# Token scaling by a diagonal matmul instead of a scaled transpose, with the norm's weights applied at the PSUM exit

## The chip, the cores and the metric

The kernel runs on one core of one Trainium2 chip. The metric is the device time of one execution in microseconds (us). A profiled execution also gives a span, from its first to its last recorded instruction.

## The reference, cut to what matters

One layer of a streaming encoder is computed for 512 prompt tokens and 64 sample tokens (576 together), each 1024 channels wide. Everything begins with one norm, whose result feeds a projection with some 13,000 columns:

```python
def _rmsnorm(x, w):
    y = x * lax.rsqrt(jnp.mean(x * x, axis=-1, keepdims=True) + EPS)
    return y * w

h = _rmsnorm(x, norm_pre_w)          # (tokens, 1024)
proj = h @ w_in                      # split into the inputs of three branches
```

The branches (a gated convolution of width 31, a state-space scan with a convolution of width 4 ahead of it, and a cross-attention) are gated, added, projected by `w_out`, normed and added to x. Only the norm at the very start is touched here.

## The kernel before, in words

**What is kept.** TensorE wants h with channels on the partitions. `hT` holds it so: 8 blocks of 128 channels by 576 tokens, once as a rounded half `hT[0]` and once as the remainder `hT[1]` (both in the type fp32r). A projection (`mac`, L218) multiplies each weight block in three parts: high weights by high h, high weights by low h, low weights by high h.

**The start.** Tokens come in five tiles, four of 128 rows and one of 64. For each, L266 issues the load of 128 x 1024 values on the SP queue. Behind the first stands L270, which loads the norm's weights repeated on all 128 partitions (`wpre`); behind the second, `prep_to(1)` issues the loads of the first two weight blocks, named B0 and C0 (L183). ScalarE rounds each weight block to its high half (`whi`, L193) and VectorE subtracts for the low half (`wlo`, L195).

**One token tile, `x_tr(t)`.** ScalarE squares the tile and sums along the row (L274) and takes the root (L275). VectorE inverts it (L276) and multiplies the tile by that column and by `wpre` in one instruction (L280). TensorE transposes eight 128 x 128 blocks into two PSUM banks, four to a bank (L291). For each bank ScalarE copies 128 x 512 into `hT[0]` (L295), and VectorE subtracts to give `hT[1]` (L296).

**The order at the start** is written out by hand, and the matmuls in it are pinned in this order:

```python
    warm_pe(16)
    x_tr(0)
    warm_pe(6)
    x_tr(1)
    warm_pe(6)
    first_mac(0, "B0")          # tokens of tiles 0 and 1
    x_tr(2)
    first_mac(0, "C0", 0, 4)
    x_tr(3)
    first_mac(0, "C0", 4, 8)
    x_tr(4)
```

Then follow the second halves (320 tokens of tiles 2, 3 and 4) of B0 and C0. `warm_pe(n)` issues n plain fp32 matmuls of the 128 x 128 identity with itself (L303); nobody reads them. PSUM tiles named `ps` come from a pool of four.

**What is not pinned** (ScalarE, VectorE, GpSimd, SP and the other matmuls) is put in order ahead of time by a planner, which walks the program by priority with costs of its own. At run time each engine takes its instructions strictly in that order.

**What comes after.** Small parameters are loaded as rows and transposed: eight of them into `vraw` (L424), transposed at L437; the weights and the state of the width-4 convolution (`scw`, `sts`) by `load_t`, through a tile `praw` with the tag `bt` of the pool `sc` (L431 load, L433 transpose, L434 copy). The tag `bt` has two buffers. The tile `after`, used by `dt_cum` (L404), has the same tag and holds one of them until then. `conv4` (L454) takes B0, C0 and then x0 to x3 through that convolution: its first ScalarE step L466 needs `scw` and, by a GpSimd copy (L459), `sts`. Beside it `dt_soft` runs a chain of small VectorE steps, whose last (L394) is what the first matmul of `dt_cum` (L402) reads. That matmul is pinned behind the projection x3. Afterwards come the chunks of the scan, with projections filled in between.

Of the kernel before, what the change touches and what calls it, by code (L numbers as in the profile page):

```python
# [8 lines left out]
F32 = mybir.dt.float32  # L9
F32R = mybir.dt.float32r  # L10
AF = mybir.ActivationFunctionType
ALU = mybir.AluOpType
# [6 lines left out]
D = 1024  # L19
# [9 lines left out]
def hybrid_trunk_kernel(  # L29
# [9 lines left out]
    nc = tc.nc  # L39
# [5 lines left out]
    const = ctx.enter_context(tc.tile_pool(name="const", bufs=1))  # L45
# [11 lines left out]
    def ps_tile():  # L57
        return pp_[1].tile([128, 512], F32, tag="ps", name="ps")


    ident = const.tile([128, 128], F32, name="ident")
# [19 lines left out]
    hT = [big.tile([128, KD, T], F32R, name=f"hT{i}") for i in range(2)]  # L81
# [156 lines left out]
    def v2(ap):  # L238
# [7 lines left out]
    sc = stc.enter_context(tc.tile_pool(name="sc", bufs=2, reuse_waits="tile"))  # L246
# [8 lines left out]
        out=mask, in_=mask, pattern=[[1, 128]], compare_op=ALU.is_ge, fill=0.0,  # L255
# [3 lines left out]
    xt = []  # L259
    for t in range(5):  # L260
        n = 128 if t < 4 else 64
        if t < 4:
            x_t = obf[:, D * t:D * t + D]
        else:
            x_t = sc.tile([128, D], F32, tag="M", name="x4")
        nc.sync.dma_start(out=x_t[:n], in_=xp_d[128 * t:128 * t + 128] if t < 4 else xs_d)  # L266
        xt.append((x_t, n))
        if t == 0:
            wpre = sc.tile([128, D], F32, tag="R", name="wpre")
            nc.sync.dma_start(out=wpre, in_=norm_pre_w[0].partition_broadcast(128))  # L270
        if t == 1:
            prep_to(1)
    def rms_tile(x_t, n, sq, ss, w):
        nc.scalar.activation(sq[:n], x_t[:n], AF.Square, accum_out=ss[:n, 0:1])  # L274
        nc.scalar.activation(ss[:n, 1:2], ss[:n, 0:1], AF.Sqrt, scale=1.0 / D, bias=eps1[:n])  # L275
        nc.vector.reciprocal(ss[:n, 2:3], ss[:n, 1:2])  # L276
        if w is None:
            nc.vector.tensor_scalar(x_t[:n], x_t[:n], ss[:n, 2:3], None, ALU.mult)
        else:
            nc.vector.scalar_tensor_tensor(x_t[:n], x_t[:n], ss[:n, 2:3], w[:n], ALU.mult, ALU.mult)  # L280

    sqx = sc.tile([128, D], F32, tag="M", name="sqx")
    ssx = const.tile([128, 5, 4], F32, name="ssx")
    def x_tr(t):
        x_t, n = xt[t]
        rms_tile(x_t, n, sqx, ssx[:, t], wpre)
        for b in range(2):
            p = ps_tile()
            for k in range(4):
                kc = 512 * b + 128 * k  # L290
                m = nc.tensor.transpose(p[:, n * k:n * k + n], x_t[:n, kc:kc + 128], ident[:n, :n])  # L291
                tc.keep_in_program_order(m)
            v = p[:, :4 * n].rearrange("p (k t) -> p k t", k=4)
            d = slice(128 * t, 128 * t + n)
            nc.scalar.activation(hT[0][:, 4 * b:4 * b + 4, d], v, AF.Copy)  # L295
            nc.vector.tensor_tensor(  # L296
                hT[1][:, 4 * b:4 * b + 4, d], v, hT[0][:, 4 * b:4 * b + 4, d].bitcast(F32), ALU.subtract
            )

    def warm_pe(n):  # L300
        p = ps_tile()
        for _ in range(n):
            tc.keep_in_program_order(nc.tensor.matmul(p[:, 0:128], lhsT=ident, rhs=ident, start=True, stop=True))  # L303
# [9 lines left out]
        )  # L313

    pt0 = {"B0": mm_tile(), "C0": mm_tile()}
    warm_pe(16)
    x_tr(0)
    warm_pe(6)
    x_tr(1)
# [11 lines left out]
    def tr_act(tiles, k, dst, wcol, ncols):  # L331
# [18 lines left out]
        out=after, in_=after, pattern=[[-1, 128]], compare_op=ALU.is_ge, fill=0.0,  # L350
# [85 lines left out]
    p = ps_tile()  # L436
# [406 lines left out]
    for kp in range(2):  # L843
# [16 lines left out]
        a, b = blk(0, 1), blk(0, 0)  # L860
        nc.vector.tensor_tensor(b, b, a, ALU.subtract)
        put("T1", b)
        c = blk(1, 1)
# [4 lines left out]
        d = blk(1, 0)  # L868
# [650 lines left out]
```

## Time and profile before

| what | value |
|---|---|
| median of 3 runs | 1129.82 us (1129.18 to 1131.78) |
| the profiled execution | 1130.53 us, span 1128.8 us |
| TensorE matmul, weight load | busy 97% and 93% of the span |
| VectorE, ScalarE, GpSimd | busy 76%, 54%, 12% |
| granted TensorE clock, mean | 0.989 |

In a row of the timeline stand the start, the time until the last of the merged instructions ended, the engine, the line, the operation, output and inputs, the count, and in brackets how long the engine had been idle and what ended that. "SPq" is the queue that issues loads. An fp32 matmul is recorded as two instructions (two passes): the 28 matmuls of `warm_pe` are 56 records at L303. Transposes and fp32r matmuls are one record each.

### The profile page before, as it was taken

The numbers are of one execution on the slowest core, as the hardware profiler recorded it, in microseconds if no ns is written. First come the engines' busy times: TensorE is split into PE (matmuls) and PEld (weight loads), VectorE is DVE, ScalarE is ACT, GpSimd is POOL, SyncE is SP. The second block draws the span as 40 slices with busy tenths as digits, with TensorE's granted clock in tenths as the row PEclk, the third lists the DMA queues.
The fourth block names the chain that finished last, engine by engine and source line by source line (L and its number), as shares of the span: only waits on it lengthen the run. The fifth ranks groups of instructions, "written<-read, shape, count | busy, mean of one in ns | idle before, by whom it ended". The sixth has DMA issues, their size and how long they took to land.

```text
span 1128.8 us, 20472 instructions
## 1 busy us (share of the span) xinstructions
PE 1091.0 (97%) x8081; PEld 1047.3 (93%) x8081; DVE 862.8 (76%) x1370; ACT 607.7 (54%) x1069; POOL 133.2 (12%) x230
## 2 busy tenths in 40 slices
PE   8999999999999999968998999999999999999997
PEld 8999999999999999968998999999899999999974
DVE  5778898578867878796888989849788789475533
ACT  5654675456437642362666576656445733674331
POOL 0100120012002100012121331100000111111000
PEclk9999999999999999988999999999999999999999
DMA  7354433442354633473867767757556889868912
GB/s 206 95 156 124 138 114 104 127 117 80 95 144 112 149 96 99 113 172 74 191 177 203 161 145 199 208 164 198 151 155 159 185 225 223 201 161 184 252 39 84
DMA packets 202213, 168.74 MB, mean 149 GB/s; under 512 B 15014, under 2 KB 175822, under 8 KB 202118
## 3 DMA queue, kind: packets, MB, share of 16 engines
q1 hardware_dynamic: 188294, 128.77, 39.4%
q0 software_dynamic: 12096, 35.13, 17.2%
q10 hardware_dynamic: 1728, 3.54, 0.8%
q8 instruction: 63, 1.03, 0.4%
q14 instruction: 32, 0.26, 0.1%
HBM read 117.08 MB, written 15.21 MB: 117 GB/s over the span
## 4 chain that ended last, share of the span: by engine, by line
PE 85%; DVE 6%; DMA 4%; ACT 2%; issue 1%; SPq 0%; DVEq 0%; ACTq 0%; POOLq 0%
PE mm L218 51%; PE X L950 9%; PE Y L950 5%; PE ps L218 4%; PE ps L1165 2%; PE ps L1166 2%; PE Z L950 2%; PE ps L1164 2%; PE ps L577 2%; PE ps L603 1%; PE ps L581 1%; DVE c L760 1%; DMA ob<-in_x_prompt_dram 1%; PE ps L542 1%; DMA wlo<-raw 1%
## 5 line engine op out<-in xcount | busy, mean ns | idle before, releaser
L218 PE MATMUL mm<-hT,whi 128*128 128x288 f32 (+2 forms) x2240 | 399.4, 298 | 1.7 <-ACT ob L689 0.7
L218 PEld LDWEIGHTS mm<-hT,whi 128*128 128x128 f32 x2240 | 334.2, 189 | 5.6 <-issue 2.2
L218 PE MATMUL mm<-hT,wlo 128*128 128x288 f32 (+2 forms) x1120 | 246.2, 298 | 0.0
L193 ACT ACTIVATE whi<-raw 128x1024 fp32r<-128x1024 f32 x118 | 124.7, 1057 | 196.5 <-PE mm L218 166.1
L760 DVE SCALAR_TENSOR_TENSOR c<-u,dww,c 128x606 f32<-128x606 f32 x240 | 202.1, 845 | 2.3
L218 PEld LDWEIGHTS mm<-hT,wlo 128*128 128x128 f32 x1120 | 184.7, 189 | 0.8 <-issue 0.6
L218 PE MATMUL mm<-hi,whi 128*128 128x288 f32 x512 | 112.2, 301 | 8.1 <-ACT hi L620 7.8
L195 DVE TENSOR_TENSOR wlo<-raw,whi 128x1024 fp32r<-128x1024 f32 x68 | 83.0, 1220 | 41.4 <-ACT whi L193 41.4
L218 PE MATMUL mm<-lo,whi 128*128 128x288 f32 x512 | 110.8, 298 | 1.6 <-DVE lo L622 1.6
L218 PE MATMUL mm<-hi,wlo 128*128 128x288 f32 x512 | 110.6, 297 | 0.8 <-DMA wlo<-raw 0.8
L218 PEld LDWEIGHTS mm<-hi,whi 128*128 128x128 f32 x512 | 83.1, 191 | 9.4 <-ACT hi L620 8.1
L198 POOL DMA_DIRECT2D wlo<-raw x50 | 43.9, 878 | 389.5 <-ACT wlo L197 286.7
L218 PEld LDWEIGHTS mm<-lo,whi 128*128 128x128 f32 x512 | 83.4, 190 | 1.9 <-DVE lo L622 1.9
L218 PEld LDWEIGHTS mm<-hi,wlo 128*128 128x128 f32 x512 | 83.2, 189 | 1.2 <-DMA wlo<-raw 1.0
L197 ACT ACTIVATE wlo<-raw 128x1024 fp32r<-128x1024 f32 x50 | 52.4, 1048 | 21.9 <-PE ps L218 21.9
L470 DVE SCALAR_TENSOR_TENSOR acc<-xp,scw,acc 128x579 f32<-128x579 f32 x72 | 58.3, 814 | 5.2 <-ACT acc L466 4.1
L917 ACT ACTIVATE ph<-rawb 128x512 fp32r<-128x512 f32 x34 | 21.5, 632 | 52.1 <-PE Z L950 22.4
L933 DVE TENSOR_TENSOR wlo<-sm,whi 128x1024 fp32r<-128x1024 f32 x34 | 41.5, 1220 | 4.5 <-ACT whi L932 4.4
L462 POOL COPY tails<-xp 128x3 f32<-128x3 f32 x24 | 18.3, 762 | 191.7 <-ACT xp L460 186.4
L932 ACT ACTIVATE whi<-sm 128x1024 fp32r<-128x1024 f32 x34 | 35.9, 1056 | 7.3 <-PE X L950 3.5
L691 DVE TENSOR_TENSOR ob<-ob,mm 128x576 f32<-128x576 f32 x24 | 18.0, 751 | 19.7 <-PE mm L218 19.6
L563 ACT ACTIVATE M<-R,tok 128x128 f32<-128x128 f32 (+1 forms) x80 | 24.8, 380 | 13.1 <-PE ps L603 13.1
(375 smaller groups left out, 2248.6 us busy)
## 6 DMA issues: line engine op xcount, KB each, us to landing
raw<-in_w_in_dram SPq DMA_DIRECT2D x70, 512.0 KB
wlo<-raw POOLq DMA_DIRECT2D x50, 512.0 KB, 5.6
raw<-in_w_in_dram SPq DMA_DIRECT2D x34, 256.0 KB
rawb<-in_w_in_dram SPq DMA_DIRECT2D x34, 256.0 KB
R<-scr SPq DMA_DIRECT2D x16, 512.0 KB
raw<-in_ssd_out_w_dram SPq DMA_DIRECT2D x16, 512.0 KB
raw<-in_xa_kv_w_dram SPq DMA_DIRECT2D x16, 512.0 KB
pl<-raw POOLq DMA_DIRECT2D x17, 256.0 KB, 3.7
```

The source lines that it names most:

```text
L193: a = nc.scalar.activation(hi[:, :n_], raw[:, :n_], AF.Copy)
L195: b = nc.vector.tensor_tensor(lo[:, :n_], raw[:, :n_], hi[:, :n_].bitcast(F32), ALU.subtract)
L197: nc.scalar.activation(lo[:, :n_], raw[:, :n_], AF.Copy, scale=-1.0)
L198: nc.gpsimd.dma_start(out=lo[:, :n_], in_=raw[:, :n_], accum_op=ALU.add)
L218: m = nc.tensor.matmul(o, lhsT=w, rhs=r[:, s:s + w_], start=(i == 0 and a == 0), stop=(i == n - 1 and a == 2),)
L470: nc.vector.scalar_tensor_tensor(acc, xp[:, r:r + 579], w4[:, r, jt:jt + 1], acc, ALU.mult, ALU.add)
L563: nc.scalar.activation(M[:, 4 + e, :], R[:nl, 4 + e, :], AF.Relu, scale=-1.0, bias=tok[:nl, 0, c, a + 4:a + 5])
L577: nc.tensor.matmul(pS, lhsT=bt[:nl], rhs=xw[:nl], start=True, stop=True)
L760: nc.vector.scalar_tensor_tensor(c, upad[j][:, r:r + NC], w31[:, r, j:j + 1], c, ALU.mult, ALU.add)
L932: nc.scalar.activation(hi, sm, AF.Copy)
L933: nc.vector.tensor_tensor(lo, sm, hi.bitcast(F32), ALU.subtract)
L950: nc.tensor.matmul(o, lhsT=w[:, k], rhs=r[:, k], start=(start and k == 0 and a == 0), stop=(k == 3 and a == 2), skip_group_check=True,)
```

## The change

The load of the repeated weights goes. In its place the 1024 weights are loaded as 8 rows of 128 (`vpr`), transposed once on TensorE (`pre_cols`, between 12 and 4 of the warm-up matmuls) and copied by VectorE into eight columns `vpre`. The token tile itself is no longer multiplied. VectorE multiplies the identity by the tile's column of inverse roots, which gives a 128 x 128 diagonal `dg` (tag `bt`), and TensorE multiplies each 128 x 128 block of x by that diagonal: the product is the transposed block, scaled by token. Where a block leaves PSUM it is multiplied by its column of `vpre`: for three blocks in four by ScalarE, for the fourth by VectorE (high half), and for all by VectorE (low half). What was two instructions of 128 x 512 for each bank becomes eight of 128 x 128.

```diff
         if t == 0:
-            wpre = sc.tile([128, D], F32, tag="R", name="wpre")
-            nc.sync.dma_start(out=wpre, in_=norm_pre_w[0].partition_broadcast(128))
+            vpr = sc.tile([8, 128], F32, tag="cbm", name="vpr")
+            nc.sync.dma_start(out=vpr, in_=norm_pre_w[0].rearrange("(j c) -> j c", c=128))
...
+    vpre = const.tile([128, 8], F32, name="vpre")
+    def pre_cols():
+        p = ps_tile()
+        tc.keep_in_program_order(nc.tensor.transpose(p[:, :8], vpr, ident[:8, :8]))
+        nc.vector.tensor_copy(vpre, p[:, :8])
...
-            nc.vector.scalar_tensor_tensor(x_t[:n], x_t[:n], ss[:n, 2:3], w[:n], ALU.mult, ALU.mult)
...
+        dg = sc.tile([128, 128], F32, tag="bt", name="dg")
+        nc.vector.tensor_scalar(dg[:n, :n], ident[:n, :n], ss[:n, 2:3], None, ALU.mult)
         for b in range(2):
             p = ps_tile()
             for k in range(4):
                 kc = 512 * b + 128 * k
-                m = nc.tensor.transpose(p[:, n * k:n * k + n], x_t[:n, kc:kc + 128], ident[:n, :n])
+                m = nc.tensor.matmul(p[:, n * k:n * k + n], lhsT=x_t[:n, kc:kc + 128], rhs=dg[:n, :n], start=True, stop=True)
                 tc.keep_in_program_order(m)
-            v = p[:, :4 * n].rearrange("p (k t) -> p k t", k=4)
-            d = slice(128 * t, 128 * t + n)
-            nc.scalar.activation(hT[0][:, 4 * b:4 * b + 4, d], v, AF.Copy)
-            nc.vector.tensor_tensor(
-                hT[1][:, 4 * b:4 * b + 4, d], v, hT[0][:, 4 * b:4 * b + 4, d].bitcast(F32), ALU.subtract
-            )
+            for k in range(4):
+                j = 4 * b + k
+                v, d = p[:, n * k:n * k + n], slice(128 * t, 128 * t + n)
+                w = vpre[:, j:j + 1]
+                if k == 3:
+                    nc.vector.tensor_scalar(hT[0][:, j, d], v, w, None, ALU.mult)
+                else:
+                    nc.scalar.activation(hT[0][:, j, d], v, AF.Copy, scale=w)
+                nc.vector.scalar_tensor_tensor(hT[1][:, j, d], v, w, hT[0][:, j, d].bitcast(F32), ALU.mult, ALU.subtract)
...
-    warm_pe(16)
+    warm_pe(12)
+    pre_cols()
+    warm_pe(4)
     x_tr(0)
```

More of the change, by code (lines that the diff above doesn't have):

```diff
@@ L268, in hybrid_trunk_kernel, with x_tr @@
         if t == 0:
-            wpre = sc.tile([128, D], F32, tag="R", name="wpre")
-            nc.sync.dma_start(out=wpre, in_=norm_pre_w[0].partition_broadcast(128))
+            vpr = sc.tile([8, 128], F32, tag="cbm", name="vpr")
+            nc.sync.dma_start(out=vpr, in_=norm_pre_w[0].rearrange("(j c) -> j c", c=128))
         if t == 1:
             prep_to(1)
-    def rms_tile(x_t, n, sq, ss, w):
-        nc.scalar.activation(sq[:n], x_t[:n], AF.Square, accum_out=ss[:n, 0:1])
+    sqx = sc.tile([128, D], F32, tag="M", name="sqx")
+    ssx = const.tile([128, 5, 4], F32, name="ssx")
+    vpre = const.tile([128, 8], F32, name="vpre")
[3 more added lines that the diff above has]
+        nc.vector.tensor_copy(vpre, p[:, :8])
+    def x_tr(t):
+        x_t, n = xt[t]
+        ss = ssx[:, t]
+        nc.scalar.activation(sqx[:n], x_t[:n], AF.Square, accum_out=ss[:n, 0:1])
         nc.scalar.activation(ss[:n, 1:2], ss[:n, 0:1], AF.Sqrt, scale=1.0 / D, bias=eps1[:n])
         nc.vector.reciprocal(ss[:n, 2:3], ss[:n, 1:2])
[L277 to L286, printed above, removed]
+        dg = sc.tile([128, 128], F32, tag="bt", name="dg")
+        nc.vector.tensor_scalar(dg[:n, :n], ident[:n, :n], ss[:n, 2:3], None, ALU.mult)
         for b in range(2):
```

## The prediction

> **What bounds the kernel now.** I read the busy shares first, then the chain that ended last, first as shares and then by time over the first 75 us, and then the timeline of the first 25 us by engine.
>
> ```profile
> PE 1091.0 (97%) x8081; PEld 1047.3 (93%) x8081; DVE 862.8 (76%) x1370; ACT 607.7 (54%) x1069; POOL 133.2 (12%) x230
> PE 85%; DVE 6%; DMA 4%; ACT 2%; issue 1%; SPq 0%; DVEq 0%; ACTq 0%; POOLq 0%
> ```
>
> TensorE (PE) bounds the kernel, and 85% of the last chain is its work. So a change at the start is worth what it moves the point from which TensorE runs without a break. The chain by time shows where that point lies now:
>
> ```profile
> 3.75 8.87 DMA ob<-in_x_prompt_dram
> 12.64 1.15 ACT sqx L274 x2
> 13.79 0.49 ACT hT L295
> 14.30 0.70 DVE hT L296
> 15.05 3.02 PE mm L218 x23
> 18.07 0.87 PE ps L291 x8
> 18.94 1.44 PE mm L218 x12
> 20.38 0.87 PE ps L291 x8
> 21.25 1.43 PE mm L218 x12
> 22.68 0.41 PE ps L291 x4
> 23.11 0.39 ACT hT L295
> 23.52 0.43 DVE hT L296
> 24.00 7.15 PE mm L218 x47
> ```
>
> Until 15.05 the start is held by the third token load, then by ScalarE's square of that tile, which stands ahead of the eviction of tile 1. From 15.05 it is TensorE's own work, with one break before 24.00 for the last tile's eviction. At 24.00 the 47 matmuls of the second halves begin; I take that as the mark, and forecast where it goes.
>
> **The change part by part.** The rows for the start are these (timeline; the last is an instruction of the kind that makes a diagonal, from later on):
>
> ```profile
> 1.59 5.71 PE L303 MATMUL ps<-ident 128*128 128x128 f32 x32 [1.59 <-POOL dtb L343]
> 5.78 0.16 DVE L276 RECIPROCAL ssx<-ssx 128x1 f32<-128x1 f32 x1 [5.78 <-ACT ssx L275]
> 6.48 1.28 DVE L280 SCALAR_TENSOR_TENSOR ob<-ob,ssx,wpre 128x1024 f32<-128x1024 f32 x1 [0.53 <-DMA wpre<-in_norm_pre_w_dram]
> 7.80 1.06 ACT L274 ACTIVATE sqx<-ob 128x1024 f32<-128x1024 f32 x1 [2.05 <-DMA ob<-in_x_prompt_dram]
> 7.82 1.09 PE L291 MATMUL ps<-ident,ob 128*128 128x128 f32 x8 [0.52 <-DVE ob L280]
> 8.75 1.50 PE L303 MATMUL ps<-ident 128*128 128x128 f32 x12
> 9.59 1.06 ACT L193 ACTIVATE whi<-raw 128x1024 fp32r<-128x1024 f32 x1 [0.31 <-DMA raw<-in_w_in_dram]
> 10.55 1.07 ACT L295 ACTIVATE hT<-ps 128x512 fp32r<-128x512 f32 x2
> 10.71 1.22 DVE L195 TENSOR_TENSOR wlo<-raw,whi 128x1024 fp32r<-128x1024 f32 x1
> 11.84 1.28 DVE L296 TENSOR_TENSOR hT<-ps,hT 128x512 fp32r<-128x512 f32 x2
> 22.61 0.71 PE L291 MATMUL ps<-ident,x 64*128 64x64 f32 x8
> 84.37 0.48 DVE L560 TENSOR_SCALAR M<-R,tok 128x128 f32<-128x128 f32 x2
> ```
>
> *The repeated load* (one SP issue, replaced by one of 4 KB at the same place in the queue). The page's list of issues and the windows give its size and the rate:
>
> ```profile
> wpre<-in_norm_pre_w_dram SPq DMA_DIRECT2D x1, 512.0 KB
> 8.00:12.00 4.00, 3.31 (x28) 2.91 (x27) 2.66 (x4) 3.65 (x7) 0.00 (x0) 1.00 1.16 338
> ```
>
> 512 KB at 338 GB/s are 1.55 us, by which all later loads come earlier: tile 1 at 6.25 instead of 7.80, B0's weights at 8.0 instead of 9.59, tile 2 at 11.1 instead of 12.6. The first tile stands ahead of it in the queue and keeps its time. VectorE's 0.53 us wait for `wpre` goes too.
>
> *The scaling.* Five VectorE instructions of 1.28 go; five products of a 128-column identity with a column come, as at L560: two in 0.48, so 0.28 long and 0.20 apart. The first diagonal is ready at 5.94 + 0.28 = 6.2 instead of the scaled tile at 7.76. But what is late next stands in the same pinned queue: the warm-up ends its issue at 1.59 + 5.71 - 0.28 = 7.03 (the 0.28 is a matmul's own latency, 1.50 less eleven spacings), and the one transposition of `pre_cols` (0.11) goes in as well. So tile 0 begins at 7.14, only 0.68 earlier than at 7.82. `pre_cols` waits for `vpr`, 4 KB that stand in the queue right behind tile 0. Tile 0 must have landed before its square of 1.06 could end ahead of 5.78, so before 4.7; 24 of the 32 warm-up records stand ahead of `pre_cols`, to about 5.7. I cost the wait at nothing, under the cover of the warm-up; without that cover each us that `vpr` lands after 5.7 would be one us on the path.
>
> *TensorE.* Eight transposes are 8 records, (0.87 for eight in the chain) 0.109 each. Eight fp32 matmuls are what `warm_pe` does: 16 records, by L303's twelve in 1.50 (less the 0.28 tail, by 11) 0.111 each: 1.78 for a tile, 0.91 more. For the 64-token tile the row L291 gives (0.71 - 0.23) / 7 = 0.069 each; sixteen cost between 1.10 (at 0.069) and 1.78 (at 0.111, if the weight load of 128 columns sets the pace); I take the middle, 1.44.
> The page "TensorE: Matmul & The Clock Gate" of the Trainium skill says in its section "Terms" that the transpose mode is four times as fast for FP32. By that a tile would cost 3.5 us instead of 1.78; the 0.111 of L303, the very form that the change issues, is two records for a matmul and no slower than a transpose in each, so here the trace says twice.
>
> *The evictions.* Rows of 128 x 128 (timeline, four of a kind each), beside L560 above:
>
> ```profile
> 72.82 1.27 ACT L563 ACTIVATE M<-R,tok 128x128 f32<-128x128 f32 x4
> 83.34 1.12 DVE L612 SCALAR_TENSOR_TENSOR xs<-xs,dcol,ps 128x128 f32<-128x128 f32 x4
> ```
>
> Spacings: ScalarE (1.27 - 0.39) / 3 = 0.29, VectorE (1.12 - 0.34) / 3 = 0.26 with two operands and 0.20 with one. A tile costs ScalarE 6 x 0.29 = 1.74 (before 1.07), VectorE 8 x 0.26 + 2 x 0.20 = 2.48 (before 1.28); with the scaling gone, VectorE has per tile 2.84 instead of 2.72. In exchange a block can be used as soon as it is out.
>
> *The start of the products, S.* For TensorE alone: 7.14 + 1.78 (tile 0) + 1.33 (warm-up) + 1.78 (tile 1) + 1.33 = 13.36. ScalarE, in the order of before: square and root of tile 1 from 6.25 to 7.7 (now from 7.80 to 9.59 less the idle 0.31); cast of B0 from 8.0 to 9.0; tile 0's evictions to 10.7; cast of C0 to 11.7; square of tile 2 to 12.9; tile 1's first block 13.2. VectorE, in the order of before: B0's subtraction 9.0 to 10.1, tile 0's low halves to 12.6, C0's subtraction to 13.7, the next diagonal to 14.0, first low half 14.3. The planner may put C0's subtraction behind; so S is 13.36 to 14.3, and with the spacings at their full durations (0.39, 0.34) about 14.5. I take 13.9 against 15.05.
>
> *The sum to the mark.* 13.9 + 3.02 (B0) + 1.78 + 1.44 + 1.78 + 1.43 + 1.44 (tile 4) + 0.1 = 24.9, against 24.00. The 0.1 is what is left of the wait for the last tile: its first blocks leave PSUM while the second bank is filled (8 of the 16 records), where now 0.39 + 0.43 follow the transposes. So TensorE gains 1.15 us at the start and 0.8 us at the last tile, and pays 0.91 twice and 1.0 for the wider tile 4: **+0.9 us**. Lower end: 13.36, 1.10 and no wait give 23.9 (-0.1). Upper end: 14.5, 1.78 and the old wait of 0.9 give 26.4 (+2.4). Finer pieces also mean more semaphore waits ahead of the first products; no row shows their price, none to 0.3 us.
>
> *From the mark on* TensorE is the chain, so the shift is carried to the end. The profiled execution (1130.53, span 1128.8) would become 1131.4. It lies 0.7 above the median of the runs, so the forecast for a median is 1129.82 + 0.9, which I round to **1130.6**. Against 0.2% (2.3 us), about what a measurement of this kernel can tell from no change, that is no change.
>
> **The rivals.**
>
> *1. The parameters of the convolution come late (slower).* The diagonals take the tag `bt`, through which `scw` and `sts` are loaded. The queue and its users now:
>
> ```profile
> 18.50 0.42 SPq L431 DMA_DIRECT2D praw<-in_ssd_conv_w_dram  x1
> 23.67 0.32 SPq L431 DMA_DIRECT2D praw<-in_state_conv_ssd_dram  x1
> 31.00 0.23 PE L433 MATMUL ps<-ident,praw 72*128 72x72 f32 x1
> 33.69 1.63 ACT L466 ACTIVATE acc<-xp,half,scw 128x579 f32<-128x579 f32 x2 [0.87 <-POOL xp L459]
> 60.98 0.33 DVE L394 SCALAR_TENSOR_TENSOR dtw<-tok,eal 128x160 f32<-128x160 f32 x1 [0.28 <-POOL tok L393]
> 61.51 0.43 PE L402 MATMUL ps<-dtw,mask 128*128 128x160 f32 x2
> 40.00:50.00 10.00, 10.00 (x77) 9.77 (x76) 8.34 (x18) 6.16 (x12) 1.84 (x8) 1.00 0.39 108
> 50.00:60.00 10.00, 10.00 (x77) 10.00 (x76) 9.48 (x20) 4.39 (x8) 2.23 (x6) 1.00 0.33 89
> ```
>
> If buffers go round in program order, the load at 18.50 waits for tile 4's last matmul (about 24), and SP's weight loads stand behind it; `sts` must then wait for the transposition of `scw`. If the planner then sets the transposition of `scw` at 31.00, `sts` is issued at 31.2 instead of 23.67, 7.6 us later, L466 comes at 41.3 at the worst, and VectorE's convolutions with it. VectorE's idle time from 40 to 60 is 1.66 + 0.52 = 2.2 us, and L394 ends 0.2 before TensorE takes its result; the rest, 5.2 us, falls on TensorE. With the forecast's 0.9 that is 1135.9. It decides from a delay of 3.8 us (0.9 + 3.8 - 2.4 = 2.3), that is L466 after 37.5. For it: the two buffers. Against it: between 18.50 and 33.69 lie 15 us, and `the transposition at 31.00 came 7.3 us after its load was issued, so most of a shift can vanish there.
>
> *2. The rest falls into another order (either side).* The planner sees other times at the start and may order the rest anew. TensorE's longest single waits (who waited for whom) bound what there is to win or lose:
>
> ```profile
> PE mm L218 <- ACT hi L620: 7.8, 1, 7.8
> ```
>
> A third of such a wait either way is 2.6 us: 1128.0 or 1133.2 with the 0.9. Nothing in the change reaches that far by data, so for each side the chance is small.
>
> *3. The matmul costs four transposes (slower).* Tiles 0 and 1 at 3.49 each put S at 16.8; 16.8 + 3.02 + 2 x 3.49 + 2.87 + 2.2 is 31.9, 7.9 after the old mark: 1137.7. It is the four-fold rule of the Trainium skill (TensorE: Matmul & The Clock Gate, Terms) taken as it stands; L303 speaks against it.
>
> **How the numbers follow.** The forecast (mark between 23.9 and 26.4, rest as before) has 0.60: 1129.7 to 1132.2. Rival 1 with 3.8 us or more has 0.12, with less it stays within the forecast's own range. Rival 2 has 0.13 for faster and 0.13 for slower. Rival 3 has 0.02. Of the forecast, all but the last tenth is under +2.3; of rival 2's slower side half crosses it. So faster 0.14, same 0.61, slower 0.25. The range 1127.4 to 1133.4 leaves out rival 3, most of rival 1 and the far ends of rival 2.
>
> **What would show it.** Right: tile 0's matmuls as 16 records of 0.11 spacing from about 7.1; the first product near 13.4 to 14.3; tiles 2 and 3 at 1.78 each; no pause before the second halves, which begin near 24.9; the first ScalarE step of `conv4` near 33 to 36. Wrong: a `dg` that waits for a buffer, a pause of TensorE for low halves of tile 1 inside B0, that step after 37.5, or a wait after 75 us that stands longer or shorter than before by more than 2 us.

## The result and the profile after

The changed kernel takes 1140.43 us (median of 6 runs, 1138.78 to 1141.36) against 1128.89 us for the kernel before in the same set: a ratio of 1.0101, 95% interval 1.0087 to 1.0115. It is slower by 11.5 us. The forecast was 1130.6 with a range up to 1133.4, so it missed. The profiled execution took 1141.25 us with a span of 1139.5, 10.7 more than the profiled execution before.

The busy shares and the shares of the last chain, from the page of the changed kernel:

```profile
PE 1095.8 (96%) x8122; PEld 1053.3 (92%) x8122; DVE 865.7 (76%) x1411; ACT 611.6 (54%) x1089; POOL 131.6 (12%) x230
PE 85%; DVE 7%; DMA 3%; ACT 2%; issue 1%; SPq 1%; DVEq 0%; ACTq 0%
```

TensorE is busy 4.8 us longer than before (1091.0) and idle 5.9 us longer (43.7 against 37.8). The chain by time (start, length, what) says where:

```profile
18.78 2.93 PE ps L309 x12
21.71 3.12 PE mm L218 x24
24.84 1.78 PE ps L294 x16
26.62 1.44 PE mm L218 x12
28.06 1.78 PE ps L294 x16
29.85 1.43 PE mm L218 x12
31.28 1.93 PE ps L294 x16
33.21 0.03 PE ps L445
33.23 1.62 DMA praw<-in_ssd_conv_w_dram
...
37.51 3.86 PE mm L218 x26
41.36 4.22 PE mm L370 x32
```

The last row is `dt_proj`, which follows the second halves of B0 and C0. The same work in the chain of the kernel before:

```profile
31.22 4.22 PE mm L362 x32
```

I call this point E, the end of C0: 41.36 against 31.22, 10.14 us later. The rest, span less E, is 1098.1 against 1097.6. So 10.14 of the 10.7 us between the two profiled executions lie in the start. The timeline shows what the start waits for (in brackets the idle time before an instruction and what ended it); ScalarE first, then VectorE, then TensorE:

```profile
6.00 1.06 ACT L285 ACTIVATE sqx<-ob 128x1024 f32<-128x1024 f32 x1 [0.22 <-DMA ob<-in_x_prompt_dram]
8.19 1.06 ACT L193 ACTIVATE whi<-raw 128x1024 fp32r<-128x1024 f32 x1 [1.04 <-DMA raw<-in_w_in_dram]
9.15 0.28 ACT L286 ACTIVATE ssx<-ssx,eps 128x1 f32<-128x1 f32 x1
...
12.04 0.61 ACT L303 ACTIVATE hT<-ps,vpre 128x128 fp32r<-128x128 f32 x2
...
13.61 1.06 ACT L285 ACTIVATE sqx<-ob 128x1024 f32<-128x1024 f32 x1 [0.78 <-DMA ob<-in_x_prompt_dram]
...
16.39 1.11 ACT L303 ACTIVATE hT<-ps,vpre 128x128 fp32r<-128x128 f32 x4
9.28 1.23 DVE L195 TENSOR_TENSOR wlo<-raw,whi 128x1024 fp32r<-128x1024 f32 x1 [2.73 <-ACT whi L193]
10.42 0.16 DVE L287 RECIPROCAL ssx<-ssx 128x1 f32<-128x1 f32 x1
10.79 1.23 DVE L195 TENSOR_TENSOR wlo<-raw,whi 128x1024 fp32r<-128x1024 f32 x1 [0.21 <-ACT whi L193]
11.93 0.28 DVE L289 TENSOR_SCALAR dg<-ident,ssx 128x128 f32<-128x128 f32 x1
...
15.05 0.61 DVE L304 SCALAR_TENSOR_TENSOR hT<-ps,vpre,hT 128x128 fp32r<-128x128 f32 x2 [1.63 <-ACT hT L303]
7.27 1.95 PE L294 MATMUL ps<-dg,ob 128*128 128x128 f32 x16
...
12.31 2.02 PE L294 MATMUL ps<-dg,ob 128*128 128x128 f32 x16 [1.76 <-issue]
18.78 2.93 PE L309 MATMUL ps<-ident 128*128 128x128 f32 x12 [4.45 <-DVE hT L304]
21.36 0.78 PE L218 MATMUL mm<-hT,whi 128*128 128x256 f32 x2
```

Three things are to be seen. First, tile 1's square is done at 7.1, but its root (9.15) stands behind the cast of B0, which waited for its load; the reciprocal then stands behind B0's subtraction and the diagonal (11.93) behind C0's, so tile 1 is transposed at 12.31. Second, ScalarE does two of tile 0's six evictions at 12.04, and next in its order come a root and the square of tile 3, which waits 0.78 us for its load; two more evictions follow at 14.66, and the last of the six ends at about 17. Third, TensorE waits until 18.78, 4.45 us long, for a low half on VectorE: the third warm-up needs a PSUM buffer, and all four hold banks of tiles 0 and 1. Then the products begin, at 21.36 (before, 15.05).

After that pause TensorE works at half the clock for 3.4 us, from 18.87 to about 22.2 (two of the windows: the columns behind the first are length, busy times of PE, PEld, DVE, ACT and POOL with counts, granted clock, DMA share and GB/s):

```profile
19.00:20.00 1.00, 1.00 (x5) 1.00 (x6) 1.00 (x5) 0.73 (x2) 0.00 (x0) 0.50 0.94 275
20.00:21.00 1.00, 1.00 (x7) 1.00 (x6) 1.00 (x5) 0.00 (x0) 0.39 (x2) 0.50 0.64 192
```

### The profile page after: what moved, and what is told of

Its sections match the earlier page's. It is cut to its first block, busy times and chain, and to the rows that moved or that the text cites. A ratio compares the mean times of both kernels' runs of the same rounds, so it can differ in the third digit from the quotient of the medians.

```text
span 1139.5 us, 20611 instructions
## 1 busy us (share of the span) xinstructions
PE 1095.8 (96%) x8122; PEld 1053.3 (92%) x8122; DVE 865.7 (76%) x1411; ACT 611.6 (54%) x1089; POOL 131.6 (12%) x230
## 4 chain that ended last, share of the span: by engine, by line
PE 85%; DVE 7%; DMA 3%; ACT 2%; issue 1%; SPq 1%; DVEq 0%; ACTq 0%
PE mm L218 52%; PE X L958 8%; PE Y L958 4%; PE ps L218 4%; PE ps L1173 2%; PE ps L1174 2%; PE ps L1172 2%; PE Z L958 2%; PE ps L585 2%; PE ps L611 1%; DVE c L768 1%; PE ps L589 1%; DMA out_dram<-ho 1%; DMA hin<-in_state_ssm_dram 1%; PE ps L550 1%
## 5 line engine op out<-in xcount | busy, mean ns | idle before, releaser
L470 POOL COPY tails<-xp 128x3 f32<-128x3 f32 x24 | 13.8, 576 | 191.3 <-ACT xp L468 191.3
```

## The experiments

I tested theory A (the order on ScalarE and VectorE and their hand-off within a bank make the start late) against C (TensorE's doubled matmuls), B (the tag `bt`, which the diagonals share with the loads of `scw` and `sts`) and D (the narrow evictions are too much work for VectorE). Each kernel is compared with runs of the kernel before on the same chip. E and the span come from each kernel's one profiled execution, the median from all its runs, and runs of one kernel differ by up to 8 us (e19: 1131.48 to 1139.78). E itself depends on when that execution's token loads landed. "Planner" is the order that the planner chose.

| kernel | what | median us | ratio, 95% | E | span - E |
|---|---|---|---|---|---|
| before | | 1128.89 | | 31.22 | 1097.6 |
| after | | 1140.43 | 1.0087-1.0115 | 41.36 | 1098.1 |
| e1 | two loops | 1133.22 | 1.0025-1.0056 | 37.83 | 1093.6 |
| e2 | own tag | 1139.19 | 1.0063-1.0118 | 40.42 | 1094.7 |
| e6 | two loops, own tag | 1135.77 | 1.0041-1.0073 | 35.91 | 1096.5 |
| e7 | e6, root of tile 1 first | 1137.48 | 1.0041-1.0091 | 37.09 | 1099.8 |
| e8 | e6 with transposes | 1130.85 | 0.9992-1.0028 | 35.86 | 1091.0 |
| e3 | wide evictions, tag `bt` | 1143.04 | 1.0101-1.0148 | 37.25 | 1104.4 |
| e9 | e3, own tag | 1131.97 | 1.0011-1.0036 | 35.21 | 1095.0 |
| e5 | before, without the load | 1130.44 | 0.9999-1.0023 | 32.23 | 1095.6 |
| e10 | first pinned order | 1133.55 | 1.0028-1.0058 | 36.09 | 1095.9 |
| e11 | e10, one loop | 1140.14 | 1.0080-1.0119 | 40.65 | 1097.8 |
| e12 | e10 with transposes | 1138.31 | 1.0058-1.0114 | 37.52 | 1100.3 |
| e13 | second pinned order | 1130.12 | 0.9996-1.0025 | 33.67 | 1094.8 |
| e14 | e13, wide evictions | 1130.34 | 0.9997-1.0028 | 33.51 | 1097.1 |
| e15 | e13 with transposes | 1130.60 | 1.0006-1.0042 | 34.06 | 1094.9 |
| e16 | e13, tag `bt` | 1130.72 | 1.0008-1.0030 | 33.48 | 1093.4 |
| e17 | e13, transposes for tiles 2-4 | 1138.31 | 1.0066-1.0109 | 36.14 | 1100.1 |
| e18 | e13, one loop | 1137.37 | 1.0051-1.0083 | 37.47 | 1096.1 |
| e19 | e17, scaling of tile 4 early | 1134.99 | 1.0035-1.0068 | 34.00 | 1099.1 |

### One part undone at a time, order left to the planner

**e1_two_loops.** In the changed kernel the four blocks of a bank go through one loop: high half, low half, next block. In the built program each next high half of the bank then waits for VectorE's low half before it. e1 splits the loop.

```diff
                 else:
                     nc.scalar.activation(hT[0][:, j, d], v, AF.Copy, scale=w)
+            for k in range(4):
+                j = 4 * b + k
+                v, w = p[:, n * k:n * k + n], vpre[:, j:j + 1]
                 nc.vector.scalar_tensor_tensor(hT[1][:, j, d], v, w, hT[0][:, j, d].bitcast(F32), ALU.mult, ALU.subtract)
```

> The changed kernel, with one edit: in each PSUM bank all four high halves are issued first and then all four low halves. Theory A (hand-off within a bank: ScalarE's copy of block k+1 waits for VectorE's low half of block k, rounds of 0.79 us): ScalarE has no waits for VectorE left at its eviction line, a bank takes about 1.0 us on ScalarE, the first product starts near 16 us instead of 21.4 and at full clock, and the time falls by 4 to 6.5 us, to 1134 to 1136.5. Rival B (the loss is the doubled TensorE passes and the order that the planner chose around them): the first product stays within 1 us of 21.4 and the time within 2 us of 1140.4.

Measured: 1133.22, 7.2 us below the changed kernel; E 37.83, 3.5 earlier. The third warm-up no longer waits for a buffer. The first product came at 18.28, later than theory A put it. In this execution the loads landed later: tile 1's square began at 7.92 instead of 6.00, and tile 2's, which stands ahead of tile 0's evictions, at 12.78 instead of 10.98. Tile 1's matmuls came behind a pause and ran at half clock.

**e2_own_tag.**

```diff
-        dg = sc.tile([128, 128], F32, tag="bt", name="dg")
+        dg = sc.tile([128, 128], F32, tag="dg", name="dg")
```

> The changed kernel, with one edit: the diagonals have a tag of their own with two buffers, so the tag bt is left to the parameters. Theory A: the loads of scw and sts are issued before 21 us instead of at 33.2 and 35.2, TensorE's pause at the transposition of scw (0.5 to 1.7 us at 34.2 to 35.2) goes, and the start of the products at 21.4 stays; time 0.5 to 1.7 us below the changed kernel, 1138.7 to 1139.9. Rival C (the late parameters hold the convolutions and are most of the loss): time falls by over 4 us.

Measured: 1139.19 and E 40.42: 1.2 us in the medians, whose intervals overlap, and 0.9 in E. TensorE's wait of 0.34 us for `scw` at 34.91 is gone; the second halves are 0.25 us shorter, and the rest of the 0.9 came before them. At most a small cost here.

**e3_wide_no_w** (the weights are left out of the computation, the evictions are 128x512 as before the change).

```diff
-                    nc.scalar.activation(hT[0][:, j, d], v, AF.Copy, scale=w)
-                nc.vector.scalar_tensor_tensor(hT[1][:, j, d], v, w, hT[0][:, j, d].bitcast(F32), ALU.mult, ALU.subtract)
...
+            nc.scalar.activation(hT[0][:, 4 * b:4 * b + 4, d], v, AF.Copy)
+            nc.vector.tensor_tensor(
+                hT[1][:, 4 * b:4 * b + 4, d], v, hT[0][:, 4 * b:4 * b + 4, d].bitcast(F32), ALU.subtract
+            )
```

> The changed kernel with the diagonal matmuls, but the norm's weights left out and each bank evicted in two instructions of 128 x 512 as before. Theory A (one hand-off a bank): first product near 16 us instead of 21.4, no half clock; time 1134 to 1136.5. Rival B (the doubled passes are the loss): 1139 to 1141.

Measured: 1143.04, though E is 4.1 us earlier than in the changed kernel. Theory A's number failed. TensorE's waits show why (us in total, times, longest):

```profile
PE ps L407 <- DVE dtw L399: 6.3, 1, 6.3
```

That is rival 1 of the prediction. From 72 to 79 the granted clock was 0.53 on average, and TensorE, at work again from 74.06, lost up to 2.3 us more by that. SP's load for `sts` goes out only after the late transposition of `scw`, VectorE's convolution follows, and `dtw` stands behind it:

```profile
37.01 0.25 PE L438 MATMUL ps<-ident,praw 96*128 96x96 f32 x1
37.28 0.33 SPq L436 DMA_DIRECT2D praw<-in_state_conv_ssd_dram  x1
41.42 0.23 PE L438 MATMUL ps<-ident,praw 72*128 72x72 f32 x1
```

**e9_wide_tag** is e3 with the tag of e2.

> e3_wide_no_w (diagonal matmuls, evictions 128x512 as before, the norm's weights left out of the computation) with the diagonal in a tag of its own. Theory B for e3's stall of 6.3 us ahead of dt_cum (scw and sts are late because their tile waits for the diagonal's buffer): the stall goes to under 2 us and the time falls by 4 to 6, to 1137 to 1139 or less. Rival R (the stall comes from the order that the planner chose after a late start, whatever the tag): 1141 to 1144, the stall of 6 us stays.

Measured: 1131.97, 11.1 below e3; the wait of 6.3 us is gone from the list, and the transposition of `scw` stands at 27.82. So theory B holds for e3's stall. In the changed kernel the same tag cost at most about 1 us.

**e5_no_load** (the kernel before without the repeated load; the weights are left out).

```diff
-            wpre = sc.tile([128, D], F32, tag="R", name="wpre")
-            nc.sync.dma_start(out=wpre, in_=norm_pre_w[0].partition_broadcast(128))
...
-        rms_tile(x_t, n, sqx, ssx[:, t], wpre)
+        rms_tile(x_t, n, sqx, ssx[:, t], None)
```

> The kernel before, without the repeated load and with the norm's weights left out; transposes and wide evictions as before. If the load's 1.5 us at the start are on the path: first product proper at 13.5 to 14.2 instead of 15.05, time 0.8 to 1.6 us below the kernel before, 1127.3 to 1128.1. If they are hidden by the order of ScalarE and VectorE: within 0.4 us of before.

Measured: 1130.44, no gain and by neither expectation; E 32.23. The loads did come earlier, but the planner then put both casts ahead of tile 0's evictions, and tile 3's square ahead of tile 1's.

**e6_two_tag** is e1 and e2 together.

> The two loops of e1_two_loops and the diagonal in a tag of its own, as in e2_own_tag. Theory A (the start is late because ScalarE and VectorE hand a bank back and forth, because the root of tile 1 stands behind the cast of B0, and because squares that wait for loads stand among the evictions): the tag adds nothing to e1, whose transposes of scw waited for no load; 1132 to 1134.5, first product near 18.4, C0's second half ends at 37 to 38. Rival B (the tag of the diagonal, shared with the tiles that the scan's setup loads into, is a cost of its own): 1 to 1.6 us below e1, 1131 to 1132.5, and scw is transposed earlier than e1's 32.36.

Measured: 1135.77, E 35.91. E is 1.9 earlier than e1's and 4.5 earlier than e2's. The 1.9 is no gain of the tag: ScalarE's order is the same in e1 and e6, and tile 2's square, which waits for its load, began at 12.78 in e1 and at 10.92 in e6, 1.86 earlier. The median is 2.5 above e1's although E is earlier: the rest of the kernel took 2.9 us longer, a first sign of the last column's spread.

**e7_root_first.**

```diff
+    stats(0)
+    stats(1)
+    first_casts(True)
     warm_pe(12)
```

`stats` holds a tile's square, root, reciprocal and diagonal; `first_casts` the casts of B0 and C0, pinned behind the root of tile 1.

> e6_two_tag with the statistics of tiles 0 and 1 traced ahead of the casts of B0 and C0, the root of tile 1 and the casts pinned in that order on ScalarE; the square of tile 2 still stands ahead of the first evictions. Theory A: the diagonal of tile 1 is ready some 1.9 us earlier (10 instead of 11.9), TensorE does tile 1 without its pause of 2.1 us and not at half clock (1.8 us instead of 3.5), but the evictions still wait for the square of tile 2, whose load lands near 13.5: first product 17.5 to 18.4, C0's second half ends 35.5 to 37.5, time 1130.5 to 1133. Rival C (the doubled time of the matmuls on TensorE, 3.6 us over the five tiles, is what the start lost): no change against e6.

Measured: 1137.48, a miss. The diagonal of tile 1 came at 9.47 and its matmuls ran without a pause, as expected; but the evictions still stood behind the square of tile 2, and the third warm-up waited 2.2 us for a buffer. That square's load landed 1.19 us later than in e6 (12.11 against 10.92), and E is 1.18 later: moving one link alone bought nothing.

**e8_tr_two.**

```diff
-        dg = sc.tile([128, 128], F32, tag="dg", name="dg")
-        nc.vector.tensor_scalar(dg[:n, :n], ident[:n, :n], ss[:n, 2:3], None, ALU.mult)
+        nc.vector.tensor_scalar(x_t[:n], x_t[:n], ss[:n, 2:3], None, ALU.mult)
...
-                m = nc.tensor.matmul(p[:, n * k:n * k + n], lhsT=x_t[:n, kc:kc + 128], rhs=dg[:n, :n], start=True, stop=True)
+                m = nc.tensor.transpose(p[:, n * k:n * k + n], x_t[:n, kc:kc + 128], ident[:n, :n])
```

> The narrow evictions with the weights as columns in two loops, as e6_two_tag, but the tokens are scaled on VectorE (one 128x1024 TENSOR_SCALAR a tile) and TensorE transposes them: the diagonal and its matmuls are undone, the columns and the missing load stay. Theory A: the scaling takes VectorE longer than the diagonal (about 1.1 us against 0.28) and the order of the squares is as bad as e6's, so the start stays late: 1131 to 1134, C0's second half ends 35.5 to 37.5. Rival C (doubled matmuls on TensorE): the whole start comes back, 1128.5 to 1130.5, C0's second half ends near 33.

Measured: E 35.86, in theory A's bounds and against rival C's 33. That it is e6's to 0.05 us is chance: the planner chose another order here (three evictions ahead of tile 2's square), TensorE waited 3.25 us for tile 1's scaling, and the granted clock was 0.50 from 12.0 to about 19, which it was not in e6. So e8 does not price the matmuls. The median, 1130.85, lies between the two ranges. The rest (1091.0, the shortest of all) makes it low, and the profiled execution, 1128.59, was 2.3 below that median.

### The order pinned

**e10_pinned, e11_pinned_one_loop, e12_tr_pinned.** Here ScalarE's order is pinned close to the one that the prediction assumed, with one difference: tile 2's square, which the prediction has ahead of tile 1's evictions, stands behind them.

```diff
+        if t == 2:
+            nc.vector.tensor_scalar(one, hT[0][:, 6, 128:129].bitcast(F32), 0.0, 1.0, ALU.mult, ALU.add)
+        a = nc.scalar.activation(sqx[:n], x_t[:n], AF.Square, scale=one if t == 2 else 1.0, accum_out=ss[:n, 0:1])
...
+                    a = nc.scalar.activation(hT[0][:, j, d], v, AF.Copy, scale=w)
+                    if t < 2:
+                        tc.keep_in_program_order(a)
...
+    stats(0)
+    stats(1)
+    first_cast(0)
     warm_pe(12)
     pre_cols()
     warm_pe(4)
     x_tr(0)
+    first_cast(1)
     warm_pe(6)
     x_tr(1)
```

> The changed kernel's arithmetic whole (diagonal matmuls, weights as columns, no repeated load), two loops of evictions, the diagonal in its own tag, and the order on ScalarE that the prediction assumed, pinned: root of tile 1, cast of B0, evictions of tile 0, cast of C0, evictions of tile 1, and only then the squares of tiles 2 to 4 (the square of tile 2 takes a scale of 1 that one more 128x1 VectorE instruction writes after tile 1's last ScalarE eviction). Theory A (the start was late by this order): first product at 13.5 to 15, C0's second half ends at 31 to 33.5 against 35.91 in e6_two_tag and 41.36 in the changed kernel; with the rest of the kernel at 1091 to 1099 as in the runs so far, 1125 to 1132, expected 1129. Rival C (TensorE's doubled matmuls are what the start lost): C0 still ends at 35 to 37, time 1132 to 1137.

> e10_pinned with the evictions of a bank in one loop again, as in the changed kernel (high and low of a block in turn), so that a ScalarE eviction waits for the VectorE eviction before it. Theory A1 (the hand-off within a bank is a cost of its own, rounds of 0.79 us against about 0.27): four banks lie ahead of the first product's end, each some 1.0 to 1.3 us longer, so C0's second half ends 3 to 5 us later than in e10_pinned, and the time is 3 to 5 us above it. Rival A2 (only the places of the root and of the squares cost; the hand-off hides beside loads and casts): within 1.5 us of e10_pinned.

> e10_pinned with transposes in place of the diagonal matmuls: the tokens are scaled by VectorE in one 128x1024 TENSOR_SCALAR a tile (0.75 us in e8_tr_two). The same order is pinned on ScalarE. Rival C: 3.6 us of doubled matmuls come back whole, C0 ends 3 to 4.5 us earlier than in e10_pinned. Theory A: before the first product the matmuls lie beside loads and casts, so only those of tiles 2 to 4 count (2 x 0.9 and about 1.0) less what their longer scaling keeps them waiting: 1 to 3 us earlier than e10_pinned, 1124 to 1130.

Measured: e10 has E 36.09 and 1133.55, outside theory A's bounds. Its first product began near 14.2, as theory A said, but then TensorE paused twice (1.18 us until 15.76, 0.48 until 17.57) for VectorE, which did tile 1's low halves behind C0's subtraction. My `one` also held ScalarE for 3.4 us. In e11 and e10 the second token load landed alike (tile 1's square at 7.29 and 7.34): E is 4.6 us later and the time 6.6 us longer, A1's way and in time more than its 3 to 5. Up to 1.7 of the 4.6 is a stretch of 3.4 us at half clock that e10 lacks. e12 missed both expectations (E later by 1.4): TensorE waited 2.8 us for tile 4's scaling, and 3.4 us at half clock followed.

**e13_order2** takes both faults out of e10.

```diff
         if t == 2:
-            nc.vector.tensor_scalar(one, hT[0][:, 6, 128:129].bitcast(F32), 0.0, 1.0, ALU.mult, ALU.add)
+            with tc.issue_after(last[0].ins):
+                nc.scalar.activation(sqx[:n], x_t[:n], AF.Square, accum_out=ss[:n, 0:1])
...
     x_tr(0)
-    first_cast(1)
     warm_pe(6)
     x_tr(1)
+    stats(2)
+    first_cast(1)
```

`last[0]` is tile 1's last eviction on ScalarE; `issue_after` sets an order on one engine and no wait.

> e10_pinned with the square of tile 2 issued behind tile 1's ScalarE evictions without a wait for VectorE, and the cast of C0 behind that square's root, so that VectorE does all low halves of tile 1 ahead of C0's subtraction. Everything else as e10_pinned. Theory D (VectorE is the chain of the start: B0's subtraction, then four banks at 1.29 us each against 0.64 of the wide form): VectorE ends tile 1's low halves 1.2 us earlier than e10 (17.8), C0's second half ends near 34.9 (e10: 36.1), time 1130 to 1134. Rival C (TensorE's doubled matmuls): C0's end as in e10, 35.8 to 36.2.

Measured: 1130.12, the ratio's interval takes in 1. The changed kernel's arithmetic, whole, costs at most 0.25% in this order and with a tag of its own. The order is not quite the assumed one either: C0's cast, too, now stands behind tile 1's evictions. E is 33.67, earlier than either theory said. The chain shows TensorE without a break:

```profile
1.59 5.38 PE ps L340 x24
...
8.21 1.79 PE ps L320 x16
10.00 1.34 PE ps L340 x12
11.34 1.79 PE ps L320 x16
13.13 1.34 PE ps L340 x12
14.47 3.13 PE mm L229 x24
...
24.05 1.93 PE ps L320 x16
...
33.67 4.21 PE mm L406 x32
```

**e18_one_loop_order2** puts the one loop back into e13.

> e13_order2 with the evictions of a bank in one loop again, as in the changed kernel, so that within a bank ScalarE's next high half waits for VectorE's low half. Theory A1: rounds of 0.79 us in place of 0.26, so tile 1's low halves end 3 to 5 us later than in e13 (16.5), C0's second half ends 3 to 5 us later than 33.67, and the time is 1133 to 1136. Rival A2 (the hand-off costs only beside a bad order): within 1.5 us of e13.

Measured: E 3.8 us later, time 7.2 above e13 (A1 for E, more than that in time), and no half clock in either start. ScalarE and VectorE in e18, and the same evictions of tile 0 in e13:

```profile
11.05 0.37 ACT L329 ACTIVATE hT<-ps,vpre 128x128 fp32r<-128x128 f32 x1 [1.30 <-DVE hT L332]
11.84 0.62 ACT L329 ACTIVATE hT<-ps,vpre 128x128 fp32r<-128x128 f32 x2 [0.42 <-DVE hT L332]
...
11.45 0.35 DVE L332 SCALAR_TENSOR_TENSOR hT<-ps,vpre,hT 128x128 fp32r<-128x128 f32 x1 [0.43 <-ACT hT L329]
12.24 0.35 DVE L332 SCALAR_TENSOR_TENSOR hT<-ps,vpre,hT 128x128 fp32r<-128x128 f32 x1 [0.43 <-ACT hT L329]
```

```profile
10.08 1.64 ACT L329 ACTIVATE hT<-ps,vpre 128x128 fp32r<-128x128 f32 x6
```

A round of one high and one low half takes 12.24 - 11.45 = 0.79 us; neither engine works while the other does. In two loops six high halves take 1.64 together. With e2, e6, e13 and e18 (all with the tag of their own) the two causes stand in a square of E and median:

| | planner's order | pinned order |
|---|---|---|
| one loop | 40.42 / 1139.19 | 37.47 / 1137.37 |
| two loops | 35.91 / 1135.77 | 33.67 / 1130.12 |

The hand-off is worth 3.8 to 4.5 us of E (of e2's 4.5 up to 1.7 is half clock behind its pause of 3.71 us), the order 2.2 to 3.0. The order's part changes with the loads: e6's landed early, and from e1 to e16, both with the tag `bt`, it is 4.35. In the medians the hand-off is 3.4 and 7.2 us and the order 1.8 and 5.7, so the two do not simply add, and part of either lies behind E.

**e14_wide_order2** (the weights left out), **e15_tr_order2**, **e16_bt_order2**: e13 with the evictions of e3, with the transposes of e8, with the tag `bt`.

> e13_order2 with evictions of 128x512 as before the change; the norm's weights are left out of the computation. Theory D: VectorE has 4 x 0.65 = 2.6 us less ahead of the last low half of tile 1; the first product runs without pauses and C0's second half ends 1.5 to 2.6 us earlier than in e13. Rival C: it ends within 0.5 us of e13.

> e13_order2 with transposes and the tokens scaled on VectorE (128x1024 TENSOR_SCALAR, 0.75 us) in place of diagonal and matmuls. Doubled matmuls cost 0.9 us each for tiles 2 and 3 and 1.5 for tile 4 (1.93 against 0.41) where they lie on the chain, 3.3 in all: by rival C, C0's second half ends 3 to 4 us earlier than in e13. Theory D: VectorE, with 0.47 us more for each tile's scaling, holds part of that back: 1.5 to 3 us earlier.

> e13_order2 with the diagonal in tag bt again, as in the changed kernel, through which scw and sts are loaded. Theory B (the tag delays scw and sts behind the last diagonal): TensorE waits 0.3 us or more for scw's load before the second halves' end, sts is transposed 6 to 8 us later than in e13, and the wait ahead of dt_cum grows; 1.5 to 7 us above e13. Rival: the 15 us of slack before conv4's first step hide it, within 1 us of e13.

Measured: E 33.51, 34.06, 33.48, medians 1130.34, 1130.60, 1130.72. None differs from e13 by more than 0.6; against the kernel before, e15 and e16 are slower by some 0.2%, with intervals that leave out 1. Theory D falls as a cause of e13's time, since in e13 TensorE waits for nobody and wide evictions gain 0.2 us of E. That 0.2 is not a clean price: e14's warm-up was faster (tile 0 at 7.11 against 8.05), and its second warm-up then waited 0.59 us for VectorE's copy of `vpre`. In e14 too TensorE ran on from 14.81. In e15 transposes gain nothing (E 0.4 later): the doubled matmuls lie on e13's chain, but with transposes TensorE waits for VectorE's scaling and low halves instead. The tag, though it moved the load of `scw` from 17.42 to 25.75, was hidden.

**e17_mix and e19_mix2** look for a version below both kernels: diagonals for tiles 0 and 1, transposes for tiles 2 to 4.

```diff
+        if t < 2:
+            dgs[t] = sc.tile([128, 128], F32, tag="dg", name="dg")
+            nc.vector.tensor_scalar(dgs[t][:n, :n], ident[:n, :n], ss[:n, 2:3], None, ALU.mult)
+        else:
+            nc.vector.tensor_scalar(x_t[:n], x_t[:n], ss[:n, 2:3], None, ALU.mult)
...
+                else:
+                    m = nc.tensor.transpose(p[:, n * k:n * k + n], x_t[:n, kc:kc + 128], ident[:n, :n])
```

In e19 the statistics of tiles 3 and 4 are traced ahead of tile 2's evictions, and their scalings are pinned.

> e13_order2 with diagonals for tiles 0 and 1 alone; tiles 2, 3 and 4 are scaled on VectorE (0.75 us each, the one of tile 2 ahead of C0's subtraction) and transposed as before. If the 2.5 us by which e13's C0 ends later than before are the doubled matmuls of tiles 2 to 4 (0.91 twice and 1.52), then C0's second half ends near 30.5 to 31.5, level with the kernel before (31.16) or up to 0.7 earlier, and the time is 1126 to 1129. Rival: VectorE's scaling of tiles 2 to 4 makes TensorE wait for about what the transposes save, C0 ends at 32.5 to 34, time 1129 to 1131.

> e17_mix with the statistics and scalings of tiles 3 and 4 traced ahead of tile 2's evictions and tile 4's scaling pinned ahead of the evictions of tile 3, so that TensorE needn't wait for it (3.1 us in e17). If the doubled matmuls of tiles 2 to 4 are what is left of the loss: C0's second half ends at 30.3 to 31.5 (e13: 33.67, before 31.16), time 1126 to 1130, even with the kernel before or a little below. Rival: VectorE's longer scaling gives it back in other waits: C0 ends after 32.5, 1129 to 1132. The order of the rest, which moved the time by up to 5 us at equal starts, can hide either.

Measured: e17 has E 36.14, 1138.31, since the planner put the scaling of tile 4 behind the evictions of tile 3:

```profile
25.18 1.11 PE L328 MATMUL ps<-ident,x 64*128 64x64 f32 x8 [3.12 <-DVE x L314]
```

e19 takes that wait away, but E is 34.00, the rival's case, and the time 1134.99, 3 us above the rival's range. TensorE's eight transposes of tile 4 were split around a wait for VectorE's low halves:

```profile
21.73 0.46 PE L328 MATMUL ps<-ident,x 64*128 64x64 f32 x4
22.93 0.46 PE L328 MATMUL ps<-ident,x 64*128 64x64 f32 x4 [0.73 <-DVE hT L343]
```

With scaling (0.75 a tile) and narrow low halves (1.29 a bank) VectorE needs 3.33 us a tile and is the slowest of the three for tiles 2 to 4. E in e19 also holds a stretch at half clock (25.3 to 28.7). In these two tries, then, the doubled matmuls were not saved: the diagonal takes work off VectorE that it did not take back without new waits. No version came below the kernel before.

## Why the prediction was wrong

**The step that failed is S, "in the order of before".** The first product was put at 13.36 to 14.3; it came at 21.36. The prediction took the durations from the rows, moved them by the load that goes, and kept the order in which ScalarE and VectorE had done them before. That order is the planner's, and it chose another one. The one loop added waits besides: the prediction allowed "none to 0.3 us" for them in all, and e18 shows 0.43 us on each side, per block. The second halves began at 33.22 in the changed kernel (24.00 before). So the 9.2 us by which E missed the forecast (10.14 less 0.9) are 7.46 for S (1.25 of it the third warm-up at half clock, 2.58 instead of 1.33), 0.87 from S to the second halves (11.86 instead of 10.99), and 0.92 in the second halves (8.14 instead of 7.22). How much of the 7.46 is the order and how much the hand-off, the square of runs above says only in part: each was worth some 2 to 4.5 us of E.

**The arithmetic held where the order was pinned without faults.** No run has the assumed order itself. e10 keeps it on VectorE: there the first low half of tile 1 began at 15.37 instead of 14.3, and tile 1's load, by its square at 7.34 instead of 6.25, accounts for 1.1 of that; but B0 then paused, which the prediction did not allow for. In e13, whose order is better than the assumed one, the first product began at 14.22 (timeline; 14.47 in the chain), which is TensorE's own 13.36 plus the 0.91 by which tile 0 began late (8.05 instead of 7.14, the warm-up of the last section); in e19 it began at 13.54. e13's time was 1130.12 against a forecast of 1130.6. By the chain its E is 2.45 later than before where 0.9 was forecast: 0.57 for S, 0.74 up to the second halves (0.49 of it tile 4) and 0.24 in them. The rest of that execution was 2.8 us shorter than in the profiled execution before, so part of the agreement in time is luck.

**The loads.** Tile 1's square was forecast at 6.25 and began at 6.00; B0's cast at 8.0, it was 8.19; tile 2's at 11.1, it was 10.98. Right in this execution, but not dependable: in kernels without the repeated load that square began anywhere between 5.7 (e5) and 8.3 (e15), and e1 and e7 against e6 show that such a shift of the loads can go straight into E in the planner's order.

**The diagonal matmul.** Sixteen records, 1.78 against 0.87 for the eight transposes: twice. The trace excludes rival 3. The Trainium skill (TensorE: Matmul & The Clock Gate, Terms) calls the transpose mode four times as fast for FP32; this trace does not agree.

**Tile 4.** I took 1.44 from between 1.10 and 1.78; the chain has 1.93. The term was mis-sized by 0.49 and lies outside its bounds: here 64 columns cost no less than the 128 of the other tiles (1.78). The upper end of the sum is also 0.2 short: with 14.5 and 1.78 its terms give 26.6, not 26.4. Nothing hangs on that.

**The evictions' prices** held: ScalarE's six in 1.64 in e13, 0.25 apart; VectorE's 0.26 apart. What was not priced was who waits for whom between them.

**Pause inside B0 for low halves, a `dg` that waits:** both were named as signs against the forecast. The first came in e10, not in the changed kernel. The second came in another form: tile 1's diagonal was ready at 12.2 instead of about 8, but it waited for VectorE, behind the subtractions of B0 and C0, not for a buffer.

**Rival 1, the tag,** was given 0.12. Its mechanism is real: in e3 the full stall of 6.3 us stood where the prediction had put it. In the changed kernel it didn't decide: TensorE waited 0.34 us for `scw`. The first step of `conv4` came at 39.49, behind the mark of 37.5, but that is the late start and no sign of the tag: it came 1.9 us ahead of E, where before it came 2.5 behind E. In e16's order the tag cost nothing.

**Rival 2, another order,** was given 0.13 on the slower side and 2.6 us. It is what happened, but in the start, not in the later waits where I looked for its size, so both the place and the size were wrong. The later part exists too: span less E runs from 1091.0 to 1100.3 in kernels whose code after the start is the same (e3's stall aside). I had bounded it by a third of one long wait, 2.6; against the kernel before it is -6.6 to +2.7. Part of this belongs to the single execution: the 31 runs of the kernel before that stood beside e13 lie between 1125.95 and 1133.47. With medians in place of spans the difference to E runs from 1095.0 (e8) to 1102.2 (e17), 1097.7 before, still more than the bound. Which order brings which time there I didn't settle. The sums of TensorE's waits after 50 us follow it in part (27.5 us before, 23.4 in e8, 28.8 in e17), and so does the granted clock: a wait of 3.4 us that ends at 606.56 in e12 is followed by half clock until about 612, where e8 has no such wait and full clock (timeline of e12; windows of e12, then of e8):

```profile
606.56 0.85 PE L991 MATMUL X<-hT,ph 128*128 128x288 f32 x2 [3.36 <-ACT ct L1062]
```

```profile
608.00:612.00 4.00, 4.00 (x18) 4.00 (x18) 4.00 (x6) 2.94 (x6) 0.24 (x1) 0.50 0.59 144
```

```profile
608.00:612.00 4.00, 4.00 (x32) 4.00 (x31) 3.96 (x7) 2.29 (x5) 0.66 (x1) 1.00 0.69 165
```

The runs of one kernel show the same: of those 31, the eleven with a mean clock of 0.992 took 1128.0 on average, the three at 0.988 or less 1132.7.

## What to carry to other kernels

Where a scheduler orders the engines, a sum made of "the old order with new durations" is a forecast for a pinned order only; read the new order out of the built program, or give the re-ordering the largest share of the chance. That holds for any edit that changes when operands become ready. When a wide two-engine step is cut into pieces, emit all pieces of the first engine for one buffer before those of the second; alternating them in program order turned two engines into one here (0.79 us a round instead of 0.26). A tile tag that is free for you may be what a later load waits for: a tag of its own cost nothing and took 11 us off one variant (e3 to e9). And before two versions of a start are compared by one execution each, look when their loads landed: here that alone moved E by 1.9 us.

## What the hardware showed that I had not expected

*Half clock after short pauses, and not after every one.* After 4.45 us of pause in the changed kernel the granted clock was 0.50 for 3.4 us. It also fell after 2.08 us in e1 (timeline, windows), but not after 2.16 us in e7 (timeline; 1.00 in its windows from 13 to 20):

```profile
13.54 3.46 PE L294 MATMUL ps<-dg,ob 128*128 128x128 f32 x16 [2.08 <-issue]
```

```profile
14.00:15.00 1.00, 1.00 (x7) 1.00 (x6) 0.27 (x2) 1.00 (x5) 0.00 (x0) 0.50 0.36 56
```

```profile
15.50 1.60 PE L333 MATMUL ps<-ident 128*128 128x128 f32 x12 [2.16 <-DVE hT L328]
```

e1's sixteen matmuls took 3.46 instead of 1.95. The Trainium skill (TensorE: Matmul & The Clock Gate, Part 1) says that half rate returns after an idle window of about 3.4 us, and that the window runs free. The 4.45 agrees with that window. The 2.08 is shorter than it, so here the trace does not agree. That 2.16 did nothing can be a matter of where the pause fell in a window that runs free; no run here shows the window itself.

*The warm-up's own pace.* The first records run at 7 per us although the granted clock reads 1.00, and the change to full pace came near 5 us in some executions and near 7 in others. The windows of e13 and of e14, in both of which TensorE has the same work up to there:

```profile
5.00:6.00 1.00, 1.00 (x6) 1.00 (x6) 0.17 (x2) 0.64 (x3) 0.00 (x0) 1.00 0.85 197
```

```profile
5.00:6.00 1.00, 1.00 (x11) 0.88 (x9) 0.30 (x2) 0.52 (x3) 0.00 (x0) 1.00 1.00 287
```

Six records against eleven. Where TensorE's pinned queue is the chain, as in e13, that moved tile 0 by 0.9 us (8.05 against 7.14 forecast; 7.11 in e14).
